# Attention of a decoder step: the scaling of q and k of the later head groups on VectorE, in halves, in place of GpSimd

## Chip, cores and metric

One core of one Trainium2 chip. The metric is the device time of one execution, in microseconds (us); lower is better. The engines are named as in the profile: PE (TensorE matmuls), PEld (its weight loads), DVE (VectorE), ACT (ScalarE), POOL (GpSimd) and SP (SyncE, here only a DMA queue).

## The reference, cut to what matters

The kernel computes one step of a two-layer decoder trunk for 1040 prompt positions (16 meta tokens and 1024 prompt tokens) and 32 sample tokens: a convolution module with its ConvFFN, then multi-head latent attention with its ConvFFN. The change lies in the prompt attention. With 16 heads, queries and keys are projected from small latents, normalised per head, and the queries' last 32 columns are rotated:

```python
q = jnp.einsum('btl,lhd->bthd', rms_norm(xn @ w_dq, q_lat_norm), w_uq)      # 64 + 32 columns a head
q_nope = rms_norm(q[..., :QK_NOPE], qnorm_nope)
q_rope = rope(rms_norm(q[..., QK_NOPE:], qnorm_rope), pos)
k_nope = rms_norm(jnp.einsum('btc,chd->bthd', c, w_uk), knorm_nope)
s = (q_nope . k_nope + q_rope . kr) * SM_SCALE; causal mask; p = softmax(s); o = p @ v
```

The RMS norm of a head is a sum of squares over its 64 (or 32) columns, a reciprocal root `rr`, and a product of the columns with `rr`. That last product, 64 columns by one number for each token and head, is what the change moves. Gains are applied later, at the transposes.

## The kernel before

The trunk runs as stages one after the other: convolution, first ConvFFN, the shared latents, prompt attention (about 1344 to 1760 us in the trace), sample attention, output projection, second ConvFFN.

Prompt attention takes the 16 heads one by one, in four groups of four. For each head `n` the loop at the end of `attention` walks the 14 steps of `values(n, 0)` and `values(n, 1)`: three matmuls give a block of scores (L1349, L1351, L1352), DVE adds the causal mask on the diagonal blocks (L1354), ACT takes the exponential (L1356), two matmuls of one line weigh the values (L1339). Between those steps other generators are advanced a step at a time: `scores(n + 1)`, the row maxima of the next head (PE L1309, DVE L1311, L1314, L1316), `shift(n + 1)` (DVE L1325), `query(n + 1)` (transposes L1279, splits on ACT and DVE, L137 and L138), `keys` (transposes L1257, splits L135 and L136), `inner` (DVE L1294).

The next group of heads is prepared by the generator `side`, advanced 1.3 steps for each step of `values` (`RATE`) from step 8 (`SIDE`) of a group's first head on: `group_k(g + 1)`, then `group_q(g + 1)`. For group 1 `group_q` has already made its ten first steps before the loop. Each of the two projects nine blocks of 128 tokens (the ninth has 64 rows) on PE, copies them and squares them on ACT (L1159, L1161, L1195 to L1198), sums the squares on DVE (L1162, L1202, L1203), takes the root by Newton steps on DVE (`rsqrt`, L255 to L260, giving `rrk` or `rrq`), and then scales, in the three pieces of `PIECES`: blocks 0 to 3, blocks 4 to 7, and block 8.

- In `group_k` the scaling of a piece is one product over 1024 columns on 128 partitions (256 columns on 64 for block 8), L1177, on POOL.
- In `group_q` the inner function `chunk` makes a piece in three steps: the scaling of the 64 plain columns of each head (L1211, by the engine given as `eng`: POOL for the later groups), the scaling of the 32 rotary columns into a scratch tile (L1217, DVE, 512 columns), and the rotation in `rope` (four products L1105 and L1108, L1109, DVE, 256 columns each). The plain and the rotary columns are apart, so L1211 and the DVE operations of the same piece don't wait for each other.

Group 0 goes another way (pieces by pairs of heads, `range(2)` loops), which stays as it is.

`finish(p)` closes a pair of heads: DMAs from POOL's queue (L1380, L1381, L1383, L1385) with a reciprocal on DVE between them (L1382), a product on POOL (L1386) and a DMA (L1387).

The order of instructions on each engine is fixed when the program is built: a planner walks a simulated time line (`schedule_with_timeline_sim`) and takes, on each engine, what is ready in the order of the program text, ahead of its place where the engine would be free. At run time each engine goes through its list in that order. PE's list alone is left as written in a few places outside attention.

Of the kernel before, what the change touches and what calls it, by code (L numbers as in the profile page):

```python
# [12 lines left out]
ALU = mybir.AluOpType  # L13
# [42 lines left out]
INN = 3  # L56
EARLY = 3
PIECES = ((128, 0, 4), (128, 4, 4), (64, 8, 1))
QROW = (96, 0)
SIDE = 8  # L60
FILLQ = 4
# [57 lines left out]
class Prog:  # L119
# [991 lines left out]
    def attention(self, es):  # L1111
        nc, a = self.nc, self.a
# [22 lines left out]
        def sub(t, m, b0, nb, lo, step, w):  # L1135
            v = t[:m, b0:b0 + nb]
            return bass.AP(v.tensor, v.offset + lo, [list(v.ap[0]), [224, 2 * nb], [step, 2], [1, w]])
# [8 lines left out]
        def group_k(g):  # L1146
            kt = st["k"] = st["k"] if g else f32([128, NB, 256], "k", ag)
            uk = part("uk", a["wuk"][:, 256 * g:256 * g + 256], 256)
            ss, rr = f32([128, 36], "ssk", al), f32([128, 36], "rrk", al)
            nc.gpsimd.memset(ss, 1.0)  # L1150
            yield
            for b0 in range(0, NB, 2):
                nb = min(2, NB - b0)
                m = 128 if b0 < 8 else 64
                ps = (ps_p if g else ps_f).tile([128, 512], F32, name="p")[:m, :256 * nb]
                for j in range(nb):
                    c0 = 128 * (b0 + j)
                    self.mm3(ps[:, 256 * j:256 * j + 256], self.cth[:, c0:c0 + m], self.ctl[:, c0:c0 + m], uk[0], uk[1])
                nc.scalar.activation(fl(kt[:m, b0:b0 + nb]), ps, AF.Copy)  # L1159
                sc = f32([128, 1024], "scr", bp)[:m, :256 * nb]  # L1160
                nc.scalar.activation(sc, ps, AF.Square)  # L1161
                nc.vector.tensor_reduce(out=ss[:m, 4 * b0:4 * b0 + 4 * nb], in_=sc.rearrange("p (a b) -> p a b", b=64), op=ALU.add, axis=AX.X)  # L1162
                yield
            self.rsqrt(al, rr, [(ALL, ss, 1.0 / DN)], [128, 36], "ka")
            nc.gpsimd.tensor_copy(self.rnew[:, 4 * g:4 * g + 4], rr[:64, 32:36])
            yield
            for p in () if g else range(2):
                for m, b0, nb in ((64, 8, 1), (128, 0, 8)):
                    v = kt[:m, b0:b0 + nb, 128 * p:128 * p + 128].rearrange("p a (c b) -> p a c b", b=64)
                    s = rr[:m, 4 * b0:4 * b0 + 4 * nb].rearrange("p (a c b) -> p a c b", c=4, b=1)[:, :, 2 * p:2 * p + 2].broadcast_to([m, nb, 2, 64])  # L1170
                    x = (nc.gpsimd if p else nc.vector).tensor_tensor(out=v, in0=v, in1=s, op=ALU.mult)
                    for early in st["half"] if p else ():
                        self.after(x, early)
                yield
            for m, b0, nb in PIECES if g else ():
                v = kt[:m, b0:b0 + nb].rearrange("p a (c b) -> p (a c) b", b=64)
                nc.gpsimd.tensor_tensor(out=v, in0=v, in1=rr[:m, 4 * b0:4 * b0 + 4 * nb].rearrange("p (a b) -> p a b", b=1)  # L1177
                                        .broadcast_to([m, 4 * nb, 64]), op=ALU.mult)
                yield

        def group_q(g):
            q = st["qn"] = f32([128, NB, 2, 224], f"q{g % 2}", au if g % 2 else ag)
# [5 lines left out]
            for b in range(NB):  # L1188
                m = 128 if b < 8 else 64
# [17 lines left out]

            def chunk(v, r, m, b0, nb, c, eng):
                s = lambda i, w: r(i).broadcast_to([m, c * nb // 2, 2, w])
                w = v(0, 160, 64)  # L1210
                x = eng.tensor_tensor(out=w, in0=w, in1=s(0, 64), op=ALU.mult)  # L1211
                for early in st.get("half", ()):
                    self.after(x, early)
                yield
                w = v(64, 64, 32)
                t = f32([128, 1024], "scr", bp)[:m, :32 * c * nb].rearrange("p (a b) -> p a b", b=32)
                nc.vector.tensor_tensor(out=t.rearrange("p (a c) b -> p a c b", c=2), in0=w, in1=s(1, 32), op=ALU.mult)  # L1217
                yield
                st["rope"] = self.rope(f32([128, 1024], "scr", bp), "q", m, slice(b0, b0 + nb), c, w[:, :, :, 0:16], w[:, :, :, 16:32],
                                       t.rearrange("p (a c) b -> p a c b", c=c))  # L1220
                yield

            for r in () if g else range(2):
                for m, b0, nb in ((64, 8, 1), (128, 0, 8)):
                    def v(lo, step, w):
                        x = q[:m, b0:b0 + nb, r]
                        return bass.AP(x.tensor, x.offset + lo, [list(x.ap[0]), [448, nb], [step, 2], [1, w]])
# [3 lines left out]
                yield "half"  # L1231
            for m, b0, nb in PIECES if g else ():
                s = lambda i: rr[:m, i, 4 * b0:4 * b0 + 4 * nb].rearrange("p (a c b) -> p a c b", c=2, b=1)
                yield from chunk(lambda lo, step, w: sub(q, m, b0, nb, lo, step, w), s, m, b0, nb, 4, nc.gpsimd)

        def group_v(g):
            uv = part("uv", a["wuv"][:, 256 * g:256 * g + 256], 256, au)
# [656 lines left out]
```

## Time and profile before

| what | us |
|---|---|
| three runs | 2752.87, 2759.51, 2760.22 |
| median | 2759.51 |
| the profiled execution, whole | 2764.96 |
| its span, first to last instruction | 2763.0 |
| PE busy in it | 2654.5 |
| DVE busy in it | 1879.3 |
| POOL busy in it | 709.8 |

The profile gives, for one execution, every instruction with its start, length and what ended the idle time before it. A line of the kernel is written L1177. Windows give the busy time of each engine in a stretch, and the clock granted to TensorE as a share of 2.4 GHz (0.50 is its lower level, 1.2 GHz). The time line of an engine merges neighbours of one kind ("x3" is three instructions in one row, whose length is from the first's start to the last's end). Instructions of DVE overlap by some 0.07 us, so that the next one may start a little before the end shown for the last.

### The profile page before, as it was taken

How to read it: one execution, taken by the hardware profiler on the slowest of the kernel's cores; microseconds unless marked ns; L12 is line 12 of the kernel's file. 1: busy time of each engine (PE TensorE's matmuls, PEld its weight loads, DVE VectorE, ACT ScalarE, POOL GpSimd, SP SyncE). 2: the span in 40 equal slices, each digit the busy share in tenths (PEclk: the TensorE clock that was granted, in tenths of full speed). 3: DMA queues.
4: the chain of work that ended last, by engine and by line, in shares of the span. 5: the costliest groups of instructions: out<-in, count | busy, mean ns of one | idle time of the engine just before them, and what ended most of it. 6: DMA issues, size and time to landing. Idle time of an engine off the chain costs nothing.

```text
span 2763.0 us, 46569 instructions
## 1 busy us (share of the span) xinstructions
PE 2654.5 (96%) x16966; PEld 2449.1 (89%) x16966; DVE 1879.3 (68%) x3485; ACT 1356.8 (49%) x3701; POOL 709.8 (26%) x1019
## 2 busy tenths in 40 slices
PE   7999998999999999999889999999999999999999
PEld 6888876999999999999767776667999999999999
DVE  8899986578888875145677777676378777775232
ACT  6777775345544553023555555576245454453010
POOL 1567663023332330001111212120023333330000
PEclk9999997999999999999889999999999999999999
DMA  4111101502222236132100001367302222226122
GB/s 142 56 41 55 39 28 43 175 30 92 90 92 91 79 120 229 41 95 92 37 10 19 24 24 32 90 202 261 140 24 90 80 80 81 80 96 244 41 87 76
DMA packets 127770, 238.24 MB, mean 86 GB/s; under 512 B 39779, under 2 KB 81141, under 8 KB 127413
## 3 DMA queue, kind: packets, MB, share of 16 engines
q1 hardware_dynamic: 103828, 200.82, 22.4%
q0 software_dynamic: 9600, 32.36, 3.1%
q10 hardware_dynamic: 14112, 2.09, 0.5%
q8 instruction: 133, 2.18, 0.3%
q14 instruction: 97, 0.79, 0.1%
HBM read 183.90 MB, written 51.31 MB: 85 GB/s over the span
## 4 chain that ended last, share of the span: by engine, by line
PE 84%; DVE 6%; ACT 5%; DMA 2%; issue 2%; SPq 0%; POOL 0%; ACTq 0%; DVEq 0%; POOLq 0%
PE ps L797 29%; PE ps L175 22%; PE pk L654 5%; PE g L419 4%; PE v L1339 4%; PE ps L846 3%; PE p L151 2%; PE ps L197 2%; PE ps L1015 1%; PE p L1349 1%; PE p L1351 1%; PE p L1352 1%; PE po L1653 1%; PE s L1309 1%; PE ps L151 1%
## 5 line engine op out<-in xcount | busy, mean ns | idle before, releaser
L135 ACT ACTIVATE wh<-raw 128x512 fp32r<-128x512 f32 (+2 forms) x256 | 191.1, 749 | 539.7 <-PE ps L175 338.2
L136 DVE TENSOR_TENSOR wl<-raw,wh 128x512 fp32r<-128x512 f32 (+2 forms) x244 | 201.5, 829 | 107.4 <-ACT wh L135 105.1
L944 DVE TENSOR_TENSOR x<-ps,x 128x1074 f32<-128x1074 f32 (+1 forms) x48 | 61.0, 1270 | 291.5 <-PE ps L175 291.3
L767 DVE SCALAR_TENSOR_TENSOR c<-ub,c,c 128x1040 f32<-128x1040 f32 (+1 forms) x176 | 225.3, 1312 | 29.5 <-ACT c L763 28.4
L669 ACT ACTIVATE qq<-pk 128x64 f32<-128x64 f32 x736 | 158.4, 244 | 67.8 <-PE pk L654 67.7
L761 POOL COPY sb<-ub 128x32 f32<-128x32 f32 x88 | 87.6, 997 | 393.3 <-DVE ub L808 353.1
L1339 PE MATMUL v<-pf,vf 128*128 128x512 f32 (+4 forms) x448 | 174.4, 473 | 11.1 <-ACT pf L1356 10.7
L663 POOL TENSOR_TENSOR sq<-sq 128x256 f32<-128x256 f32 (+4 forms) x229 | 140.1, 620 | 102.1 <-ACT sq L658 95.1
L1356 ACT ACTIVATE pf<-p 128x512 f32<-128x512 f32 (+4 forms) x224 | 99.1, 450 | 118.0 <-DVE p L1354 97.4
L175 PE MATMUL ps<-xh,wh 128*128 128x358 f32 (+1 forms) x672 | 148.1, 329 | 9.2 <-ACT xh L135 5.9
L669 ACT ACTIVATION_READ_ACCUMULATOR qq<-pk 128x1 f32 x736 | 154.2, 228 | 0.0
L523 DVE SCALAR_TENSOR_TENSOR a<-u,c,a 128x512 f32<-128x512 f32 x216 | 150.2, 747 | 4.9 <-ACT a L516 4.9
L175 PE MATMUL ps<-xl,wh 128*128 128x358 f32 (+1 forms) x672 | 147.8, 328 | 0.1
L175 PE MATMUL ps<-xh,wl 128*128 128x358 f32 (+1 forms) x672 | 147.3, 327 | 0.0
L175 PE MATMUL ps<-al,wh 128*128 128x358 f32 (+1 forms) x672 | 147.2, 327 | 0.0
L175 PE MATMUL ps<-ah,wl 128*128 128x358 f32 (+1 forms) x672 | 146.5, 326 | 0.0
L175 PE MATMUL ps<-ah,wh 128*128 128x358 f32 (+1 forms) x672 | 146.2, 326 | 0.0
L654 PE MATMUL pk<-ukh,ch 128*128 128x512 f32 x256 | 115.3, 451 | 26.1 <-ACT ch L135 13.6
L763 ACT ACTIVATE c<-ub,c 128x1074 f32<-128x1074 f32 (+1 forms) x88 | 101.5, 1187 | 60.0 <-DVE ub L808 46.3
L175 PEld LDWEIGHTS ps<-xh,wh 128*128 128x128 f32 x672 | 117.2, 191 | 12.8 <-ACT xh L135 6.8
L658 ACT ACTIVATE sq<-pk 128x512 f32<-128x512 f32 x164 | 99.8, 613 | 50.3 <-PE pk L654 47.5
L135 ACT ACTIVATE wh<-s 128x512 fp32r<-128x512 f32 x120 | 75.6, 630 | 93.5 <-PE ps L797 86.7
(599 smaller groups left out, 9111.5 us busy)
## 6 DMA issues: line engine op xcount, KB each, us to landing
raw<-wup SPq DMA_DIRECT2D x88, 512.0 KB, 3.6
pg<-ctn SPq DMA_DIRECT2D x128, 192.0 KB, 3.8
raw<-wdn SPq DMA_DIRECT2D x32, 448.0 KB, 3.4
raw<-pw SPq DMA_DIRECT2D x24, 512.0 KB, 3.9
d_a<-c POOLq DMA_DIRECT2D x22, 537.0 KB, 3.5
raw<-d_a SPq DMA_DIRECT2D x22, 537.0 KB, 5.1
d_a<-c POOLq DMA_DIRECT2D x22, 531.0 KB, 3.2
raw<-d_a SPq DMA_DIRECT2D x22, 531.0 KB, 5.3
```

The costliest lines, as they stand in the source:

```text
L135: return (nc.scalar.activation(h, src, AF.Copy), (eng or nc.vector).tensor_tensor(out=l, in0=src, in1=h.bitcast(F32), op=ALU.subtract))
L136: (eng or nc.vector).tensor_tensor(out=l, in0=src, in1=h.bitcast(F32), op=ALU.subtract))
L175: nc.tensor.matmul(p[:, c, :ch], s[:, k * 128:(k + 1) * 128], m[k][:, off + c * ch:off + (c + 1) * ch], start=k == 0 and i == 0, stop=k == ...
L419: y = nc.tensor.matmul(p[:, 0], x[:, k * 128:(k + 1) * 128], m[k][:, t * ch:t * ch + ch], start=k == 0 and i == 0, stop=k == KD - 1 and i ...
L523: nc.vector.scalar_tensor_tensor(out=p[:, :ND] if j == n - 1 else acc, in0=x[:, j:j + ND], scalar=w[:, j:j + 1], in1=to if j == 1 else acc ...
L654: x = nc.tensor.matmul(ps, s[:, j, :], m[:, 512 * c:512 * c + 512], start=i == 0, stop=i == 2)
L663: nc.gpsimd.tensor_tensor(out=to, in0=v[:, :, :n], in1=v[:, :, n:2 * n], op=ALU.add)
L669: nc.scalar.activation(q, ps[:, 64 * h:64 * h + 64], AF.Square, accum_out=ss[:, p, 8 * c + h:8 * c + h + 1])
L763: x = nc.scalar.activation(c, ub, AF.Copy, scale=wd[:, t, 2:3])
L767: nc.vector.scalar_tensor_tensor(out=c[:, 2:pe], in0=ub[:, tap:tap + pe - 2], scalar=wd[:, t, tap:tap + 1], in1=c[:, 2:pe], op0=ALU.mult, ...
L797: nc.tensor.matmul(ps, w[:, s], m[:, lo:hi], start=first and k == 0 and i == 0, stop=k == KD // 2 - 1 and i == 2, skip_group_check=True)
L1339: nc.tensor.matmul(o[:, at_:], vf[:m, b, c], p[:m, :512 - at_], start=b == 0, stop=last)
```

## The change

The three pieces of the key scaling become five (blocks 0 and 1, 2 and 3, 4 and 5, 6 and 7, 8), on DVE, each a step of the generator. The scaling of the plain query columns goes to DVE too; its pieces of four blocks are cut into two instructions of 512 columns, with the generator's step between the two, and the step that stood after the scaling falls away for these pieces, so that the second half and L1217 stand in one step. Group 0, and the last block of the later groups, keep one instruction and their steps. The keys of a group now take two steps more in `side`, the queries as many as before.

```diff
+HALVES = ((128, 0, 2), (128, 2, 2), (128, 4, 2), (128, 6, 2), (64, 8, 1))
...
-            for m, b0, nb in PIECES if g else ():
+            for m, b0, nb in HALVES if g else ():
                 v = kt[:m, b0:b0 + nb].rearrange("p a (c b) -> p (a c) b", b=64)
-                nc.gpsimd.tensor_tensor(out=v, in0=v, in1=rr[:m, 4 * b0:4 * b0 + 4 * nb].rearrange("p (a b) -> p a b", b=1)
+                nc.vector.tensor_tensor(out=v, in0=v, in1=rr[:m, 4 * b0:4 * b0 + 4 * nb].rearrange("p (a b) -> p a b", b=1)
                                         .broadcast_to([m, 4 * nb, 64]), op=ALU.mult)
                 yield
...
             def chunk(v, r, m, b0, nb, c, eng):
                 s = lambda i, w: r(i).broadcast_to([m, c * nb // 2, 2, w])
-                w = v(0, 160, 64)
-                x = eng.tensor_tensor(out=w, in0=w, in1=s(0, 64), op=ALU.mult)
+                w, z = v(0, 160, 64), s(0, 64)
+                n = c * nb // 2
+                for lo, hi in ((0, n // 2), (n // 2, n)) if c == 4 and nb > 1 else ((0, n),):
+                    if lo:
+                        yield
+                    x = eng.tensor_tensor(out=w[:, lo:hi], in0=w[:, lo:hi], in1=z[:, lo:hi], op=ALU.mult)
                 for early in st.get("half", ()):
                     self.after(x, early)
-                yield
+                if c == 2 or nb == 1:
+                    yield
...
             for m, b0, nb in PIECES if g else ():
                 s = lambda i: rr[:m, i, 4 * b0:4 * b0 + 4 * nb].rearrange("p (a c b) -> p a c b", c=2, b=1)
-                yield from chunk(lambda lo, step, w: sub(q, m, b0, nb, lo, step, w), s, m, b0, nb, 4, nc.gpsimd)
+                yield from chunk(lambda lo, step, w: sub(q, m, b0, nb, lo, step, w), s, m, b0, nb, 4, nc.vector)
```

For the later groups `st["half"]` is empty, so no added edge hangs on these instructions.

## Rows read from the trace of the kernel before

**Rows 1.** Page, busy time of each engine, share, instructions

```profile
PE 2654.5 (96%) x16966; PEld 2449.1 (89%) x16966; DVE 1879.3 (68%) x3485; ACT 1356.8 (49%) x3701; POOL 709.8 (26%) x1019
```

**Rows 2.** Page, the chain that ended last, by engine

```profile
PE 84%; DVE 6%; ACT 5%; DMA 2%; issue 2%; SPq 0%; POOL 0%; ACTq 0%; DVEq 0%; POOLq 0%
```

**Rows 3.** Windows: length, busy PE, PEld, DVE, ACT, POOL, clock, DMA share, GB/s

```profile
1440.00:1465.00 25.00, 23.04 (x111) 16.04 (x110) 21.39 (x80) 13.18 (x31) 5.15 (x6) 1.00 0.02 6
...
1540.00:1570.00 30.00, 29.59 (x152) 23.60 (x151) 21.09 (x90) 19.24 (x54) 5.27 (x7) 1.00 0.00 1
1570.00:1600.00 30.00, 25.31 (x116) 17.70 (x115) 27.82 (x87) 14.03 (x32) 11.56 (x12) 0.94 0.12 37
...
1680.00:1700.00 20.00, 16.41 (x59) 10.76 (x59) 17.71 (x49) 5.52 (x14) 10.14 (x11) 0.83 0.10 28
```

**Rows 4.** Time line of POOL: start, length, instruction [idle before, releaser]

```profile
1421.65 4.33 POOL L1211 TENSOR_TENSOR q<-q,rrq 128x1024 f32<-128x1024 f32 x3 [12.16 <-DVE rrq L260]
...
1458.98 4.33 POOL L1177 TENSOR_TENSOR k<-k,rrk 128x1024 f32<-128x1024 f32 x3
...
1575.42 5.24 POOL L1211 TENSOR_TENSOR q<-q,rrq 128x1024 f32<-128x1024 f32 x3 [0.36 <-DVE mx L1316]
1580.61 0.58 POOL L1383 DMA_DIRECT2D d_l<-lq  x1
...
1587.51 2.37 POOL L1386 TENSOR_TENSOR o<-o,lb 128x1024 f32<-128x1024 f32 x1 [3.85 <-DMA lb<-d_l]
...
1682.59 4.33 POOL L1211 TENSOR_TENSOR q<-q,rrq 128x1024 f32<-128x1024 f32 x3
```

**Rows 5.** Time line of DVE after the queries' root of group 2

```profile
1575.43 0.67 DVE L1217 TENSOR_TENSOR scr<-q,rrq 128x512 f32<-128x512 f32 x1
...
1577.02 1.13 DVE L1105 TENSOR_TENSOR scr<-scr,tabqcos 128x256 f32<-128x256 f32 x1
1578.08 2.87 DVE L1105 TENSOR_TENSOR scr<-scr,tabqsin 128x256 f32<-128x256 f32 x2
1580.87 0.41 DVE L1105 TENSOR_TENSOR scr<-scr,tabqcos 128x256 f32<-128x256 f32 x1
1581.20 0.17 DVE L1354 TENSOR_TENSOR p<-p,trit 128x16 f32<-128x16 f32 x1
...
1585.07 0.75 DVE L1105 TENSOR_TENSOR scr<-scr,tabqsin 128x256 f32<-128x256 f32 x2
...
1588.50 1.66 DVE L1109 TENSOR_TENSOR q<-scr 128x256 f32<-128x256 f32 x1
```

**Rows 6.** Time line of DVE after the queries' root of group 3

```profile
1682.74 4.74 DVE L1217 TENSOR_TENSOR scr<-q,rrq 128x512 f32<-128x512 f32 x1
```

**Rows 7.** Time line of PE: the long idle times of groups 2 and 3

```profile
1581.65 0.40 PE L1339 MATMUL v<-pf,vf 128*128 128x16 f32 x2 [2.90 <-ACT pf L1356]
...
1687.68 0.50 PE L1349 MATMUL p<-qh,kth 104*128 104x512 f32 x1 [2.41 <-DVE s L1294]
```

**Rows 8.** Windows of 1 us after each of those idle times, columns as above

```profile
1583.00:1584.00 1.00, 1.00 (x4) 0.47 (x2) 1.00 (x3) 0.95 (x3) 0.66 (x2) 0.50 0.21 29
...
1691.00:1692.00 1.00, 1.00 (x3) 0.81 (x4) 1.00 (x3) 0.98 (x3) 0.00 (x0) 0.50 0.04 8
```

**Rows 9.** Time line of DVE: the whole-piece scaling in group 0

```profile
1388.40 1.21 DVE L1211 TENSOR_TENSOR q<-q,rrq 128x1024 f32<-128x1024 f32 x1
```

**Rows 10.** Windows of 5 us around the preparation of group 1, columns as above

```profile
1430.00:1435.00 5.00, 5.00 (x26) 3.48 (x24) 2.17 (x7) 2.84 (x7) 0.00 (x0) 1.00 0.00 0
...
1445.00:1450.00 5.00, 4.10 (x19) 2.89 (x19) 5.00 (x19) 3.11 (x8) 0.68 (x2) 1.00 0.01 3
1450.00:1455.00 5.00, 4.26 (x25) 3.24 (x24) 5.00 (x20) 1.08 (x4) 0.00 (x0) 1.00 0.07 24
```

**Rows 11.** Time line of DVE: idle times after the keys' roots (groups 1, 2)

```profile
1465.94 0.17 DVE L1354 TENSOR_TENSOR p<-p,trit 16x16 f32<-16x16 f32 x1 [1.80 <-PE p L1352]
...
1556.01 0.48 DVE L1202 TENSOR_REDUCE ssq<-scr 128x2 f32<-128x128 f32 x2 [1.67 <-ACT scr L1198]
```

## Prediction

> **What bounds the kernel now.** I read the page's busy shares first, then its chain, then windows over prompt attention, then the time lines of POOL, DVE and PE where a window shows PE short of work. PE is busy for 96% of the span [rows 1] and holds 84% of the chain [rows 2], so a change on DVE and POOL is worth only what PE's idle times, or its clock, have to do with those engines. The windows show where that is [rows 3]. While the keys of group 2 are made, PE is busy for 29.59 of 30 us. In the next 30 us, where group 2's queries are scaled and rotated, PE has 25.31 and the mean clock falls to 0.94; in the 20 us where group 3's are, it has 16.41 at a clock of 0.83. Idle time there is 4.7 and 3.6 us, and the lowered clock is worth 30 x 0.06 = 1.8 and 20 x 0.17 = 3.4 us: 13.5 us in all, the most that could be won in these two places. In both, DVE is nearly full (27.82 of 30, 17.71 of 20).
>
> Why DVE is full there is seen in its time line beside POOL's. In group 3 one L1217 of 512 columns takes 4.74 us [rows 6]; its twin in group 2 takes 0.67 [rows 5]. The long one lies over POOL's three L1211, 4.33 us from 1682.59 on [rows 4]. In group 2 the same POOL work starts at 1575.42, just ahead of a chain of L1105: one of 1.13 us and a pair of 2.87, where a clean single takes 0.41 and a clean pair 0.75 [rows 5]. So DVE's products whose two inputs both lie in SBUF stand still while POOL's products run: 4.74 - 0.67 = 4.07 us in group 3, (1.13 - 0.41) + (2.87 - 0.75) = 2.84 us in group 2. Behind them in DVE's list stands a causal mask (L1354 at 1581.20) or an `inner` (L1294), for which PE waits by way of the exponential or directly: its 2.90 and 2.41 us of idle time [rows 7]. After each, the clock stands at 0.50, the lower of its two levels, for some microseconds [rows 8]. The keys' scalings (L1177) and group 1's queries, as long on POOL [rows 4], run where PE has no such gap.
>
> **The change part by part.**
>
> *Removed from POOL:* L1177 and L1211 of three groups, about six times 4.33 us [rows 4]. POOL is busy for 26% [rows 1] and none of that is on the chain [rows 2], so its own time is worth nothing. What counts is the standstill of DVE: 2.84 + 4.07 = 6.9 us.
>
> *Added to DVE:* a whole piece takes 1.21 us there [rows 9]; a half of 512 columns is priced by L1217, 0.67 us, and the 256 columns of the last block by L1105, 0.41 us [rows 5]. Keys: 4 x 0.67 + 0.41 = 3.1 us a group; queries the same. That is 6.2 us a group and 18.5 us in all, 2.7 times the standstill removed. The added work is worse for DVE's total; it has to be won by place.
>
> The two instructions of a pair cost 1.34 against 1.21 us, 0.13 us more. The Trainium skill, VectorE: DVE Perf Modes, section The TRN2 errata, says that VectorE pays a fixed latency for each instruction, so that small tiles pay more often: that speaks against halves, and 12 pairs at 0.13 make the 1.6 us already in the 18.5.
>
> *Group 2's queries.* Ahead of the late mask now stand the first piece's two halves, 1.34 us, in place of 2.84 us of standstill: the mask is 1.5 us earlier, and of PE's 2.90 us about 1.4 stay. The second piece and the small one, 1.34 + 0.41 = 1.75 us, come later in a stretch where DVE is still behind; between nothing and 1.75 I take 0.5, since PE is busy again there.
>
> *Group 3's queries.* 4.07 - 1.34 = 2.7 us earlier, more than the 2.41 us of PE's wait, so I count 2.4; what is late next is the mask after it, and again 0.5 of 1.75 for the rest.
>
> How long this standstill is decides the sum. The row has it as long as all three POOL products. The Trainium skill, SBUF — State Buffer, section SBUF: two separate sides, says that a VectorE instruction with two SBUF inputs and a GpSimd instruction that reads SBUF lock each other out, whoever starts first holding the ports for its whole instruction. By that L1217 should have waited for one product, not three; at a third of 4.33 us group 3 would gain nearly nothing, and my sum would be 2 us less. The row decides.
>
> *The clock.* If the idle times shrink, the fall after them may not come: between 0 and 1.8 us in group 2, 0 and 3.4 in group 3. In group 2 a gap of half the length stays, so 0; in group 3 I take half, 1.7.
>
> *Keys of groups 2 and 3.* 3.1 us each, at a time when PE is full and DVE has 21.09 of 30 us [rows 3], with idle times such as 1.67 us just behind [rows 11]. Cover: those gaps, some 9 us in the window. Without it, masks and row maxima queue behind the scalings, and the price is the whole 3.1. In halves no mask waits for more than 0.67 us at once. I take 0.3 each, bounds 0 and 3.1.
>
> *Group 1, keys and queries.* Here DVE is tightest: from 1445 to 1455 it has no idle time and PE already loses 0.90 + 0.74 us [rows 10]. The query scalings are ready early (POOL begins at 1421.65 [rows 4]) and DVE has 2.83 us free of 5 at 1430 [rows 10], so the planner can set them there. The keys' come at 1459 [rows 4], with a gap of 1.80 us soon after [rows 11]. Together 21.39 + 6.2 = 27.6 us stand against a window of 25 [rows 3]. Bounds 0 and 6.2; I take 1.0, nearer to the free ends.
>
> *POOL's queue.* L1383 of `finish` stands behind the L1211 of group 2 until 1580.61; with these gone it goes some 3 us sooner, and L1386 (2.37 us), a product like the others, comes forward. It stops DVE now as well (an L1109 of 1.66 us where 0.41 is usual, at 1588.50 [rows 5]); moved onto other products with two SBUF inputs it can cost up to 2.37 instead of 1.25, or nothing: -1.25 to +1.1 us, taken as 0.
>
> *Steps.* Two more steps of `side` at 1.3 a step move the queries of a group back by 1.5 steps of some 14 a head; they are needed some ten steps later, so that costs nothing unless they become the last thing `query` waits for.
>
> *Sum:* -1.5 + 0.5 - 2.4 + 0.5 - 1.7 + 0.6 + 1.0 = -3.0 us. The profiled execution is 2763.0 us of span and 1.96 outside, 2764.96, which is 5.45 above the median of the three runs, 2759.51. It would come to 2762; against the median the forecast is 2756.5.
>
> **The rivals.**
>
> *The clock stays up.* Both idle times go far enough that no fall follows: -1.5 - 2.4 - 1.8 - 3.4 and no cost of the keys, -9.1 us, 2750.4. For it: the falls come right behind these two idle times and nowhere in the 1540 to 1570 window [rows 3, 8]. Against: the 1.4 us that stay in group 2, and that the scalings themselves now stand on the path.
>
> *DVE takes over (slower).* In each head that prepares a group, the added products stand ahead of masks in a list that runs in order; PE waits for masks through ACT. It decides when the gaps of DVE are not where the planner puts the halves, which shows first in group 1, where 27.6 us stand against 25. If all of it were exposed: 18.5 - 6.9 = +11.6 us, 2771; if two thirds, +8 and 2767. For it: DVE is already full beside PE's small losses at 1445 to 1455 [rows 10]. Against: the 9 us free in 1540 to 1570.
>
> *The loss only changes its name.* The masks now wait for scalings on DVE instead of a standstill, and L1386 lands worse: -1.5 - 2.4 + 3.5 + 1.6 + 1.1 = about +2 us, 2762. For it: DVE's total rises.
>
> *The planner's order turns elsewhere.* A change of engine alters its simulated time line, and lists further on may be set otherwise: no row prices this; I give it -10 to +10, nearest to the 5 us that single stalls are worth here.
>
> **How the numbers follow.** A measurement of this kernel tells about 0.3% from no change, 8.3 us: faster means below 2751.2, slower above 2767.8. The forecast has 0.52 (its own range 2751 to 2763), the clock 0.16, DVE taking over 0.16, the renamed loss 0.10, the planner 0.06. Faster: 0.12 of the clock's, 0.04 of the forecast's, 0.03 of the planner's, 0.19. Slower: 0.11 of DVE's, 0.03 of the planner's, 0.01 of the renamed loss, 0.15. The rest is 0.66. The range leaves out the outer parts of the two far cases: 2747 to 2768.
>
> **What would show it.** Right: no L1217 or L1105 of over 1 us beside L1211; the idle times before L1339 and L1349 in groups 2 and 3 under 1.5 us; clock above 0.9 in group 3's window; DVE's busy time up by about 18.5 - 6.9 = 11.6 us; POOL's down by 26. Wrong: masks that wait for DVE in heads 0 and 1, where group 1 is made, PE idle times of over 1 us there or beside the keys, or query transposes that come later than the rotation allowed before. A change of over 10 us in either direction would mean that the planner moved work that I have not looked at.

## The result, and the profile of the changed kernel

| | before | changed |
|---|---|---|
| median of 22 runs each, us | 2758.23 | 2761.61 |
| lowest to highest, us | 2751.60 to 2764.65 | 2755.34 to 2771.07 |
| profiled execution, us | 2764.96 | 2771.07 |
| its span, us | 2763.0 | 2769.2 |

The ratio is 1.0018, with an interval of 1.0010 to 1.0026: by it the changed kernel is 2.8 to 7.2 us slower (the medians differ by 3.4). That is less than the 0.3% I had named as the measurement's limit, but the sign is plain by this interval, and it is not the sign of the forecast, -3.0 us. How far such an interval holds from one set of runs to the next is seen below, at the kernel that was run two times. The profiled execution of the changed kernel is the slowest of its 22.

Lines behind the change stand six further on (L1360 for L1354, L1331 for L1325), those just ahead of it one (L1106 for L1105) and L1211 is L1216. The page of the changed kernel, busy times and the chain, against [rows 1, 2]:

```profile
PE 2655.6 (96%) x16966; PEld 2449.3 (88%) x16966; DVE 1889.6 (68%) x3515; ACT 1357.2 (49%) x3701; POOL 683.7 (25%) x1001
...
PE 81%; DVE 7%; ACT 5%; DMA 3%; issue 2%; POOL 0%; SPq 0%; ACTq 0%; DVEq 0%; POOLq 0%
```

DVE is busy for 10.3 us more (11.6 expected), POOL for 26.1 less (26 expected). So the work moved as priced, and the standstill went with it. The time line of DVE in the changed kernel, after the root of group 2's queries, against [rows 5]:

```profile
1584.40 1.29 DVE L1216 TENSOR_TENSOR q<-q,rrq 128x512 f32<-128x512 f32 x2
1585.61 0.69 DVE L1223 TENSOR_TENSOR scr<-q,rrq 128x512 f32<-128x512 f32 x1
1586.21 1.62 DVE L1216 TENSOR_TENSOR q<-q,rrq 128x512 f32<-128x512 f32 x3
...
1588.78 0.41 DVE L1106 TENSOR_TENSOR scr<-scr,tabqcos 128x256 f32<-128x256 f32 x1
...
1590.91 2.58 DVE L1109 TENSOR_TENSOR q<-scr 128x256 f32<-128x256 f32 x1
...
1600.32 1.20 DVE L1331 TENSOR_TENSOR qh<-p,pick 8x1024 fp32r<-8x1024 f32 x1
...
1604.85 0.22 DVE L1109 TENSOR_TENSOR q<-scr 64x64 f32<-64x64 f32 x1
1604.99 0.21 DVE L1110 TENSOR_TENSOR q<-scr 64x64 f32<-64x64 f32 x1
```

The L1106 has its clean 0.41 us where before it took 1.13. All five scalings of the plain query columns (L1216, two and three) stand in one stretch of 3.4 us with one L1223 between them, though the generator's steps lie between them in the program: the planner drew them together, so the halves spread nothing here. One standstill remains: an L1109 of 2.58 us, under `finish`'s product on POOL, 1.66 before [rows 5]. New is the end of the list. The last rotation product of the group starts at 1604.99, 4.7 us *behind* the `shift` (L1331, 1600.32) of the head that runs then; before, it started 3.1 us ahead of that `shift`:

```profile
1592.02 0.21 DVE L1109 TENSOR_TENSOR q<-scr 64x64 f32<-64x64 f32 x1
...
1595.16 1.20 DVE L1325 TENSOR_TENSOR qh<-p,pick 8x1024 fp32r<-8x1024 f32 x1
```

`shift` marks each head once, so the time from one `shift` to the next is the time of a head. I count heads from 0 and call "head 6" the time from the seventh `shift` to the eighth. Heads 2, 3, 8, 12 and 13 repeat within 0.1 us in most kernels, which makes these times a finer measure than the whole. Head 4 takes 27.5 or 27.9 us in most, and head 14, from 25.4 to 30.0 us, is left out. In us:

| head | 0 | 1 | 4 | 5 | 6 | 7 | 9 | 10 | 11 | 0 to 13 |
|---|---|---|---|---|---|---|---|---|---|---|
| before | 25.2 | 23.8 | 27.5 | 30.0 | 27.5 | 22.7 | 30.0 | 28.7 | 22.7 | 355.2 |
| changed | 26.7 | 24.8 | 27.9 | 30.9 | 25.6 | 25.4 | 30.2 | 25.2 | 25.4 | 359.1 |

The standstills lay in heads 6 and 10. These won 1.9 and 3.6 us. Heads 7 and 11, right behind, lost 2.7 and 2.7, heads 5 and 9 lost 0.9 and 0.2, and heads 0 and 1, where group 1 is made, 1.5 and 1.0. The profiled executions differ by 6.2 us. Of this 3.9 lie here. Another 3.4 lie ahead of the first `shift`: the shared latents start 5.5 us later in the changed kernel's execution, though up to attention every engine has the same instructions in the same order, so that this part is no effect of the change. From the end of head 13 to 1960 us of the kernel before, from where on the lists are the same again, the changed kernel takes 3.2 us more, and behind that 4.2 less.

What makes heads 7 and 11 longer is the clock. First windows of the kernel before, from head 6's standstill and then from head 7 (columns as in [rows 3]):

```profile
1578.00:1583.00 5.00, 2.10 (x10) 1.53 (x9) 5.00 (x12) 1.59 (x4) 3.58 (x4) 0.97 0.01 2
1583.00:1588.00 5.00, 5.00 (x13) 3.02 (x12) 3.67 (x13) 1.82 (x4) 1.16 (x3) 0.69 0.43 107
...
1595.00:1600.00 5.00, 3.98 (x24) 2.89 (x21) 4.94 (x15) 3.92 (x9) 0.08 (x1) 1.00 0.01 3
1600.00:1605.00 5.00, 4.70 (x27) 3.68 (x28) 3.50 (x17) 1.72 (x7) 0.42 (x1) 1.00 0.00 1
```

And the changed kernel, two windows of head 6, then two of head 7, and two of head 11:

```profile
1585.00:1590.00 5.00, 5.00 (x20) 3.44 (x19) 5.00 (x13) 3.07 (x6) 1.06 (x2) 1.00 0.37 108
1590.00:1595.00 5.00, 4.25 (x16) 2.36 (x14) 5.00 (x11) 1.10 (x3) 3.24 (x2) 1.00 0.06 25
...
1600.00:1605.00 5.00, 3.66 (x16) 2.83 (x15) 4.81 (x13) 2.19 (x5) 0.50 (x1) 0.78 0.00 0
1605.00:1610.00 5.00, 4.45 (x13) 2.59 (x11) 2.86 (x12) 2.44 (x6) 0.00 (x0) 0.54 0.02 4
...
1709.00:1714.00 5.00, 3.76 (x15) 2.68 (x15) 4.81 (x17) 2.93 (x7) 0.51 (x1) 0.80 0.00 1
1714.00:1719.00 5.00, 4.99 (x15) 3.04 (x15) 2.33 (x10) 1.34 (x5) 0.00 (x0) 0.52 0.00 0
```

The hole of 2.90 us is gone and the clock of head 6 stays at 1.00. In head 7, PE now has 3.66 of 5 us and the clock falls to 0.78 and then 0.54; 5 x 0.22 + 5 x 0.46 = 3.4 us of full clock are lost there, and before none. PE's time line of the changed kernel shows what it lacks ahead of that fall, and the twin in head 11:

```profile
1595.18 0.66 PE L1263 MATMUL s<-c,k 128*128 128x128 f32 x4 [0.93 <-DVE m L1320]
...
1601.58 0.50 PE L1355 MATMUL p<-qh,kth 128*128 128x512 f32 x1 [1.34 <-DVE qh L1331]
...
1710.02 0.51 PE L1355 MATMUL p<-qh,kth 128*128 128x512 f32 x1 [1.34 <-DVE qh L1331]
```

Both are waits for DVE, for a row maximum and for the `shift` itself. In DVE's list both stand behind rotation products of this group, whose end now reaches into the next head. That these waits bring the fall is argued and not shown: in the kernel with group 1 as before, below, PE waits the same 1.34 us for the `shift` in head 11, the rotation ends 4.7 us behind that `shift` as well, and the clock of the head stays at 1.00.

### The profile page after: what moved, and what is told of

It is laid out like the page before. It is cut to its first block, busy times and chain, and to the rows that moved or that the text cites. A ratio compares the mean times of both kernels' runs of the same rounds, so it can differ in the third digit from the quotient of the medians.

```text
span 2769.2 us, 46583 instructions
## 1 busy us (share of the span) xinstructions
PE 2655.6 (96%) x16966; PEld 2449.3 (88%) x16966; DVE 1889.6 (68%) x3515; ACT 1357.2 (49%) x3701; POOL 683.7 (25%) x1001
## 4 chain that ended last, share of the span: by engine, by line
PE 81%; DVE 7%; ACT 5%; DMA 3%; issue 2%; POOL 0%; SPq 0%; ACTq 0%; DVEq 0%; POOLq 0%
PE ps L798 27%; PE ps L176 22%; PE pk L655 5%; PE g L420 4%; PE v L1345 4%; PE ps L847 3%; PE p L152 2%; PE ps L198 2%; PE ps L1016 1%; PE p L1355 1%; PE p L1358 1%; PE p L1357 1%; PE s L1315 1%; PE po L1659 1%; PE ps L152 1%
## 5 line engine op out<-in xcount | busy, mean ns | idle before, releaser
L768 DVE SCALAR_TENSOR_TENSOR c<-ub,c,c 128x1040 f32<-128x1040 f32 (+1 forms) x176 | 225.6, 1314 | 30.9 <-ACT c L764 30.1
```

What stands on the lines that cost most here:

```text
L768: nc.vector.scalar_tensor_tensor(out=c[:, 2:pe], in0=ub[:, tap:tap + pe - 2], scalar=wd[:, t, tap:tap + 1], in1=c[:, 2:pe], op0=ALU.mult, ...
```

## The experiments

Three theories stood at the start. A: the loss moved from POOL's standstill to DVE's own added work at the end of a group. B: the two steps added to `side` by cutting the keys' scaling in five push the queries' root back, by 2.9 us, into the next head's work. C: group 1 pays.

The table has the time of heads, the start of the queries' root (last line of `rsqrt`) counted from the `shift` that opens head 5 (9), and the ratio to the kernel before with its interval. All from one profile each but the ratio. "Halves" and "whole" say how VectorE's scalings are cut.

| kernel | 1 | 5 | 6 | 7 | 9 | 10 | 11 | 0 to 13 | root g2, g3 | ratio |
|---|---|---|---|---|---|---|---|---|---|---|
| before | 23.8 | 30.0 | 27.5 | 22.7 | 30.0 | 28.7 | 22.7 | 355.2 | 37.4, 36.5 | |
| changed | 24.8 | 30.9 | 25.6 | 25.4 | 30.2 | 25.2 | 25.4 | 359.1 | 40.3, 39.6 | 1.0018 (1.0010 to 1.0026) |
| keys only | 24.6 | 30.8 | 26.6 | 27.1 | 30.2 | 26.8 | 24.7 | 361.9 | 40.2, 39.6 | 1.0035 (1.0022 to 1.0048) |
| queries only | 23.8 | 30.0 | 26.3 | 22.7 | 30.1 | 26.0 | 27.4 | 357.5 | 37.5, 36.6 | 1.0005 (0.9996 to 1.0015) |
| group 1 as before | 23.8 | 30.8 | 25.2 | 26.5 | 30.2 | 25.1 | 23.1 | 355.6 | 40.2, 39.6 | 1.0003 (0.9994 to 1.0012) |
| whole, steps of before | 24.7 | 30.0 | 26.4 | 22.7 | 31.1 | 24.3 | 23.2 | 353.8 | 37.4, 37.6 | 0.9991 (0.9980 to 1.0002) |
| two empty steps | 23.8 | 30.8 | 26.6 | 24.6 | 30.2 | 26.8 | 24.7 | 358.5 | 40.2, 39.6 | 1.0035 (1.0023 to 1.0047) |
| halves, three steps | 24.8 | 30.0 | 28.0 | 22.7 | 30.9 | 24.4 | 23.2 | 355.6 | 38.9, 37.4 | 1.0039 (1.0026 to 1.0052) |
| the same again | 24.8 | 30.0 | 26.3 | 22.7 | 30.9 | 24.4 | 23.2 | 353.7 | 37.5, 37.4 | 1.0007 (0.9994 to 1.0020) |
| RATE 1.39 | 24.6 | 30.2 | 26.2 | 22.7 | 31.0 | 24.4 | 23.2 | 355.8 | 37.6, 37.5 | 0.9998 (0.9988 to 1.0008) |
| whole, one key step | 24.7 | 34.2 | 25.0 | 22.7 | 33.4 | 25.0 | 22.7 | 359.2 | 30.9, 29.5 | 1.0010 (0.9999 to 1.0021) |
| whole, groups 2 and 3 | 23.8 | 30.0 | 26.2 | 22.7 | 30.7 | 24.3 | 23.2 | 352.1 | 37.4, 37.2 | 0.9982 (0.9971 to 0.9992) |
| RATE 1.39, group 1 as before | 23.8 | 30.2 | 26.2 | 22.7 | 31.0 | 24.4 | 24.8 | 356.0 | 37.7, 37.5 | 0.9993 (0.9981 to 1.0005) |
| no plain scaling | 24.0 | 30.0 | 23.9 | 22.7 | 30.0 | 23.3 | 22.7 | 348.2 | 37.4, 36.5 | 0.9957 (0.9944 to 0.9970) |

**Keys only** (the changed kernel with the queries back on POOL):

```diff
-                for lo, hi in ((0, n // 2), (n // 2, n)) if c == 4 and nb > 1 else ((0, n),):
+                for lo, hi in ((0, n // 2), (n // 2, n)) if eng is not nc.gpsimd and c == 4 and nb > 1 else ((0, n),):
...
-                if c == 2 or nb == 1:
+                if eng is nc.gpsimd or c == 2 or nb == 1:
...
-                ... s, m, b0, nb, 4, nc.vector)
+                ... s, m, b0, nb, 4, nc.gpsimd)
```

> Only the keys' scaling of the later groups goes to VectorE in five instructions; the queries' stays on GpSimd as before. Theory A (the loss moved: the changed kernel wins some 1.9 and 3.6 us where GpSimd no longer stops VectorE's rotation, in heads 6 and 10, and gives back 2.7 us in each of the heads 7 and 11, because the queries' products now end later on VectorE than the transposes that need them): the keys alone cost little, within 1.5 us of before, the long L1217 and L1105 beside GpSimd's L1211 are still there, and heads 7 and 11 take as long as before (22.7 us from shift to shift). Theory B (the two more steps that the keys take push the queries back): heads 7 and 11 lose some 2.7 us each here too, 4 to 6 us over before. Theory C (group 1 is the dearer part): 1 us or more is lost in head 1 by its keys.

It is slower than the whole change. The root comes 2.8 us later in group 2, and the standstill of [rows 5] is back, in DVE's time line:

```profile
1582.39 1.26 DVE L1106 TENSOR_TENSOR scr<-scr,tabqcos 128x256 f32<-128x256 f32 x1
1583.57 2.87 DVE L1106 TENSOR_TENSOR scr<-scr,tabqsin 128x256 f32<-128x256 f32 x2
```

So the half of the change that I had priced at 0.6 us for two groups carries the loss, and it is found in heads 7 and 11 again. That fits B, and speaks against A, by which the queries' scalings should be the dear ones.

**Queries only** (the changed kernel with the keys as before: `PIECES`, on POOL, three steps):

```diff
-            for m, b0, nb in HALVES if g else ():
+            for m, b0, nb in PIECES if g else ():
...
-                nc.vector.tensor_tensor(out=v, in0=v, in1=rr[:m, 4 * b0 ...
+                nc.gpsimd.tensor_tensor(out=v, in0=v, in1=rr[:m, 4 * b0 ...
```

> Only the queries' plain columns of the later groups go to VectorE in halves; the keys' scaling stays on GpSimd in three pieces with three steps. Theory A: all of the changed kernel's pattern is here, heads 6 and 10 shorter by 1.9 and 3.6 us than before, heads 7 and 11 longer by 2.7 each, group 1's query products in head 0 costing some 1.5 us; 2 to 5 us over before in all. Theory B: with the steps as before the queries come in time, heads 7 and 11 are as before, and the kernel is 2 to 4 us faster than before.

The root is back in place, and group 2 gains: head 6 1.2 us less, head 7 unchanged. Group 3 doesn't: head 10 wins 2.8 us and head 11 loses 4.7, though its root is where it was before. In time it is level with the kernel before, where B wanted 2 to 4 us less and A 2 to 5 more. In PE's time line there:

```profile
1706.88 0.50 PE L1355 MATMUL p<-qh,kth 128*128 128x512 f32 x1 [2.32 <-DVE qh L1331]
```

This head is A's case, and B doesn't explain it. The fall of the clock right behind that idle time, to 0.70 and 0.50 in windows of 5 us, comes with most of its price.

**Group 1 as before** (in the changed kernel, `g > 1` decides between the new form and the old; `chunk` as in keys only):

```diff
-            for m, b0, nb in HALVES if g else ():
+            for m, b0, nb in (HALVES if g > 1 else PIECES) if g else ():
...
-                nc.vector.tensor_tensor(out=v, ...
+                (nc.vector if g > 1 else nc.gpsimd).tensor_tensor(out=v, ...
...
-                ... s, m, b0, nb, 4, nc.vector)
+                ... s, m, b0, nb, 4, nc.vector if g > 1 else nc.gpsimd)
```

> The changed kernel with group 1's keys and queries left on GpSimd in whole pieces; groups 2 and 3 as changed. Theory C (group 1 pays: its query products stand ahead of masks in head 0 while TensorE's clock is still at its lower level, and its keys fill VectorE in head 1): 2.5 us are won back against the change, so about 2 us over before, and the clock from 1420 to 1430 us is as before. Theory A alone: the same 2.5 us, with heads 6, 7, 10 and 11 as in the changed kernel. If group 1 costs nothing: as the changed kernel, 5 us over before.

Head 1 is at 23.8 us again, so C has a size: 1.0 us there. It stands or goes with the keys' scaling of group 1 in all 13 profiles with the whole work (24.6 to 24.8 with it on VectorE, 23.8 without). Head 0 can't be charged: it takes 26.2 to 26.9 us in every kernel but the one before (25.2), those included that leave group 1 alone. Head 11 is an exception to B: its root is as late as in the changed kernel, and it is 0.4 us over before.

**Whole pieces, steps of before** (the kernel before, only the two engine names changed):

```diff
-                nc.gpsimd.tensor_tensor(out=v, in0=v, in1=rr[:m, 4 * b0 ...
+                nc.vector.tensor_tensor(out=v, in0=v, in1=rr[:m, 4 * b0 ...
...
-                ... s, m, b0, nb, 4, nc.gpsimd)
+                ... s, m, b0, nb, 4, nc.vector)
```

> Both scalings on VectorE, but in whole pieces of four blocks with the steps of before: three steps for the keys, one product of 1024 columns (1.21 us) for a pair of halves (1.34 us). Theory A: as the changed kernel, 3 to 6 us over before; longer products ahead of masks cost about what the saved 1.6 us give. Theory B: with the steps as before heads 7 and 11 lose nothing and the kernel is 1 to 3 us below before.

The same work on the same engine as in the change, without its steps: head 6 wins 1.1 us, head 10 4.4, heads 7 and 11 lose 0 and 0.6, head 9 1.1. In time it is level with the kernel before or a little better. A is refuted as the main cause: the added DVE work as such doesn't make the kernel slower.

**Two empty steps** (the kernel before, with two steps added that do nothing):

```diff
                                         .broadcast_to([m, 4 * nb, 64]), op=ALU.mult)
                 yield
+                if b0 < 8:
+                    yield
```

> The kernel before, GpSimd and all, with nothing added but two empty steps in each later group's keys, so that the projections of the queries start 1.5 steps of the values later. Theory B: the root of the queries is 2.9 us later after the shift of head 5 and heads 7 and 11 lose some 2 to 4 us each against before: 4 to 9 us over before without any work moved. Theory A: within 1.5 us of before.

Nothing is moved to VectorE, and the kernel is as slow as with the keys' half of the change: 6.3 to 13 us by its interval, which is of one set of six runs. Heads 5, 9 and 11 have the change's times or nearly (30.8, 30.2, 24.7), head 7 is 2.0 us up. Windows behind the `shift` of head 7 and of head 11 in this kernel:

```profile
1593.00:1598.00 5.00, 3.60 (x18) 2.64 (x19) 4.69 (x11) 3.78 (x10) 0.27 (x1) 1.00 0.01 3
1598.00:1603.00 5.00, 5.00 (x21) 3.55 (x20) 2.92 (x12) 1.30 (x5) 0.23 (x1) 0.66 0.00 1
...
1707.00:1712.00 5.00, 4.94 (x19) 3.56 (x20) 2.79 (x14) 1.55 (x5) 0.47 (x1) 0.66 0.01 1
```

The clock falls to 0.66 in each. So two steps without any work bring the fall to these heads, and this is B by itself. It also corrects a reading: heads 6 and 10 are 0.9 and 2.0 us *shorter* here, with the products still on POOL, so a part of what the changed kernel won there was only put off into the next head. Over the whole of these two heads the clock is 1.00 here and was 0.94 and 0.88 before, with the standstill in both kernels. From the start of head 5 to the end of head 11 the two steps cost 2.0 us; of the 3.3 over attention, 1.0 lies in head 0, which can't be charged.

The wait at the end of head 6 can be followed. In the time lines of POOL, DVE and PE:

```profile
1585.51 2.34 POOL L1388 TENSOR_TENSOR o<-o,lb 128x1024 f32<-128x1024 f32 x1 [3.53 <-DMA lb<-d_l]
```

```profile
1585.92 2.21 DVE L1108 TENSOR_TENSOR q<-scr 128x256 f32<-128x256 f32 x1
...
1588.26 0.51 DVE L1316 TENSOR_REDUCE m<-s 128x1 f32<-128x352 f32 x1
...
1590.99 0.21 DVE L1109 TENSOR_TENSOR q<-scr 64x64 f32<-64x64 f32 x1
...
1592.64 1.20 DVE L1327 TENSOR_TENSOR qh<-p,pick 8x1024 fp32r<-8x1024 f32 x1
```

```profile
1588.82 0.65 PE L1259 MATMUL s<-c,k 128*128 128x128 f32 x4 [1.96 <-DVE m L1316]
```

The delayed rotation product L1108 (clean 0.41 us) is held under `finish`'s product on POOL, the row maximum comes behind it, and PE stands for 1.96 us. The rotation itself ends 1.6 us *ahead* of the `shift` here: the late root brings the loss without the rotation reaching into the next head.

**Halves, in three steps** (the changed kernel, the halves of one piece in one step), run two times:

```diff
-                yield
+                if b0 not in (0, 4):
+                    yield
```

> The changed kernel with the keys' five products in three steps instead of five: a step stands behind each pair of halves and behind the small piece, as before the change. Theory B (the two added steps push the queries' root back by 1.5 steps of the values, 2.9 us, and their products past the transposes of the next group): the queries' root comes some 37.5 us after the shift of head 5 (40.3 in the changed kernel), the rotation ends at about 53 us instead of 61, heads 7 and 11 lose under 1 us, and the kernel is 1 to 3 us below before, like the kernel with whole pieces. Theory A (the added products on VectorE fill the end of the group whatever the steps): heads 7 and 11 together still lose 4 us or more, and it stays 4 to 6 us over before.

> The run of three key steps once more, the same kernel: it was timed 10.7 us over the kernel before, of which its profile has only 0.4 inside attention. If the rest lies in a stage order that this kernel always has, 2767 us again, ratio 1.004, and 159 to 160 us from the last shift to the end of the first part of sample attention where before has 155. If it was the spread from execution to execution, within 3 us of before, ratio 1.000 to 1.001.

Heads 7 and 11 are back at 22.7 and 23.2 in both, which B wants. The first time the kernel was timed 10.7 us over the one before, the second time 2 us (-1.7 to +5.5). The two intervals don't meet, so an interval of one set of runs is narrower than the spread between sets; the times of "keys only" and of the two empty steps, of five and six runs that were not repeated, are to be read with that, and the argument goes by the heads. The profiles, 14.7 us apart as a whole, show one source of the spread, 1.9 us of it. One program, and in head 6 the windows of the first profile, then those of the second:

```profile
1574.00:1578.00 4.00, 3.28 (x11) 1.98 (x10) 2.23 (x11) 1.77 (x5) 1.08 (x2) 0.68 0.01 1
...
1586.00:1590.00 4.00, 4.00 (x9) 2.12 (x9) 4.00 (x14) 1.67 (x3) 1.05 (x2) 0.62 0.47 131
```

```profile
1569.00:1573.00 4.00, 3.27 (x18) 2.15 (x17) 3.32 (x19) 2.54 (x7) 1.08 (x2) 1.00 0.01 1
...
1581.00:1585.00 4.00, 4.00 (x15) 2.37 (x14) 4.00 (x15) 0.60 (x1) 0.48 (x1) 1.00 0.48 124
```

PE is as busy in the one as in the other (3.28 and 3.27, then 4.00 and 4.00 of 4 us), and the clock falls in one alone: 28.0 against 26.3 us for the head, which is most of the 1.9. A single head time of a single profile is therefore good to some 1.7 us where a fall is near, not to 0.1. What carries B is the count. In the four kernels with the late root (39.6 to 40.3 us), seven of the eight heads 7 and 11 are 1.9 us or more over before; in the eight other profiles with the whole work, whose root is at its old place within 1.5 us or earlier, it is two of sixteen (head 11 of "queries only" and of the RATE kernel with group 1 as before).

**RATE 1.39** (the changed kernel; `side` goes faster, so that five steps take no longer than three did), and **with group 1 as before** on top:

```diff
-RATE = 1.3
+RATE = 1.39
```

> The changed kernel with the generator advanced 1.39 steps for each step of the values in place of 1.3, so that its 32 steps take the time that 30 took. Theory B: the root of the queries is back at about 37.5 us after the shift of head 5, and the 5 us of the change are won back: between 3 us below and 1 over before. Theory A: still 4 to 6 us over before.

> The changed kernel with group 1 back on GpSimd and RATE 1.39 in place of 1.3, so that the keys' five steps take no longer than three did. Theory B and C: heads 0 and 1 as before, heads 7 and 11 at 22.7 and 23.3 us as in the run with RATE 1.39 alone, about 353.5 us from first to last shift, 1.7 us under the kernel before: ratio 0.9994. Theory A: heads 7 and 11 stay near 25.4 us, ratio 1.001.

The root is back at 37.6 and the loss in heads 7 and 11 with it (22.7, 23.2), in the first; in time it is the kernel before again, since heads 4 and 8 pay 1.5 and 0.5 us for the faster `side`. In the second, head 11 had a fall of the clock once more, and the gain that I expected over the first is within the interval. As a number it is a miss, 356.0 us for 353.5.

**Whole pieces, keys in one step** (the kernel with whole pieces and the steps of before, with two steps fewer):

```diff
-                yield
+                if b0 == 8:
+                    yield
```

> Whole pieces on VectorE for both, and the three products of the keys in one step instead of three, two steps fewer than before. Theory B carried on: the queries' root comes another 2.9 us sooner, 34.5 us after the shift of head 5, and the end of the group gets slack: 2 to 6 us below before. If the steps of before are already early enough: as with whole pieces, 1 to 3 us below before; if the three products of the keys in one place stand ahead of masks, up to 2 us worse than that.

Earlier isn't better either, and the expectation missed: the root comes at 30.9 and 29.5 us for the 34.5 expected, the time is +2.8 us (-0.3 to +5.8) for -2 to -6, heads 6 and 11 are as short as in any kernel with the whole work, but heads 5 and 9 pay 4.2 and 3.4 us for the work that now falls into them.

**No plain scaling.** The kernel before without the product L1211 of groups 1 to 3; what it computes for these heads lacks that factor.

```diff
-                x = eng.tensor_tensor(out=w, in0=w, in1=s(0, 64), op=ALU.mult)
+                if c == 2:
+                    x = eng.tensor_tensor(out=w, in0=w, in1=s(0, 64), op=ALU.mult)
```

> The kernel before without the scaling of the plain query columns of groups 1 to 3 (left out altogether, on GpSimd as on VectorE), its steps kept: what the change could win at most at the queries if VectorE's halves cost nothing. All theories: the standstills go, heads 6 and 10 fall by 2 and 4 to 5 us; B says that heads 7 and 11 stay at 22.7, so 348 to 350 us from first to last shift against 355.2, ratio 0.9975 to 0.998. If heads 7 and 11 rise here as well, the loss there isn't from VectorE's work or the steps but from what follows when the standstill goes.

This is the ceiling: heads 6 and 10 fall by 3.6 and 5.5 us and heads 7 and 11 don't move, 7.0 us over attention and 8 to 15 in time, more than the 5.5 to 7 expected. Taking the standstill away has no loss of its own behind it.

**Whole pieces, groups 2 and 3 alone** (steps of before, group 1 on POOL):

```diff
-                nc.gpsimd.tensor_tensor(out=v, in0=v, in1=rr[:m, 4 * b0 ...
+                (nc.vector if g > 1 else nc.gpsimd).tensor_tensor(out=v, in0=v, in1=rr[:m, 4 * b0 ...
...
-                ... s, m, b0, nb, 4, nc.gpsimd)
+                ... s, m, b0, nb, 4, nc.vector if g > 1 else nc.gpsimd)
```

> The kernel before, with the scalings of keys and queries of groups 2 and 3 alone as whole pieces on VectorE, one step each as before; group 1 stays on GpSimd. Theory B and C together (the lock at the queries costs, the added steps and group 1's move give the gain back): heads 0 and 1 as before (25.2 and 23.8 us from shift to shift), heads 6 and 10 as in the run of whole pieces for all groups (26.4 and 24.3 us against 27.5 and 28.7), 352.3 us from first to last shift against 355.2, so 2.5 to 3 us under the kernel before: ratio 0.999. Theory A (the added VectorE work costs at the group's end whatever the steps): 355 us or more, ratio 1.000 to 1.002.

Expected were 352.3 us over attention, found 352.1; the median of 12 runs is 2751.55 us, the ratio 0.9982 (0.9971 to 0.9992). By its interval, of one set of runs, it is faster than the kernel before, by 5 us, and its ratio lies below the changed kernel's. The end of its rotation and the next `shift` in DVE's time line, and windows of its head 7:

```profile
1590.49 1.75 DVE L1105 TENSOR_TENSOR scr<-scr,tabqcos 64x64 f32<-64x64 f32 x1
...
1593.35 0.20 DVE L1109 TENSOR_TENSOR q<-scr 64x64 f32<-64x64 f32 x1
...
1596.98 1.20 DVE L1325 TENSOR_TENSOR qh<-p,pick 8x1024 fp32r<-8x1024 f32 x1
```

```profile
1597.00:1602.00 5.00, 3.81 (x23) 2.83 (x21) 4.94 (x15) 3.99 (x10) 0.25 (x1) 1.00 0.02 3
1602.00:1607.00 5.00, 4.87 (x27) 3.81 (x28) 3.43 (x18) 1.65 (x7) 0.25 (x1) 1.00 0.00 1
```

The rotation ends 3.6 us ahead of the `shift`, much as before, and the clock holds. In group 3 it ends 1.6 us ahead, no more than with the two empty steps, and the clock of head 11 holds as well.

## Why the prediction was wrong

**The step that failed** is "Steps". It had the size right: 1.5 steps, and the root came 2.9 us later in group 2 (40.3 against 37.4). It priced them at nothing, since the queries "are needed some ten steps later". That looked at when the queries are needed, and not at where their products stand in DVE's list. The runs give the price. From the start of head 5 to the end of head 11 the kernel before takes 189.3 us and the changed kernel 190.4. The same halves with the keys in three steps, and so with the root in its place, take 186.9 and 185.3, and with five steps and a faster `side` 186.0. So the two steps cost 3.4 to 5.1 us in these heads, where the rest of the change won 2.4 and 4.0. In the kernel before, without any work moved, they cost 2.0.

How the late root costs that is shown in part only. In the changed kernel the rotation ends 4.7 us behind the `shift` of head 7, where before it ended 3.1 ahead, with DVE at 27.82 of 30 us [rows 3]. But a used-up slack is not what the late kernels share: with keys only and with two empty steps the rotation ends 1.6 us ahead of the `shift`, as it does ahead of that of head 11 in five profiles whose clock holds there. What the four share, in both groups, is the product that `finish` holds up: one of 256 columns on 128 partitions, for 2.2 to 2.6 us. With the whole work and the root in its old place it is one of 64 columns on 64 partitions, for 1.1 to 2.0 us (in group 2 of the kernel before one of 256, for 1.66), and with the keys in one step none. No run moves the one without the other, and head 11 of "group 1 as before" has both and no fall. What the falls in heads 7 and 11 hang on stays open.

**The removed standstill** came out in size, but not as reckoned. With the steps as before, VectorE's scalings make head 6 shorter by 1.1 to 1.3 us (but for the profile with the fall of the clock) and head 10 by 2.8 to 4.4; the sum had 1.0 for group 2 and 2.4 - 0.5 + 1.7 = 3.6 for group 3. Of that, PE's idle time in the two heads was to fall by 2.9 us and fell by 1.9 (8.4 before, 6.5 in the second profile with halves in three steps), and the clock was counted with 1.7 and gave more: 0.94 and 0.88 over the two heads before, worth 1.7 and 3.4 us, and 1.00 in both after. The two empty steps raise it to 1.00 there with the standstill in place, so that the clock's part can't be put down to the standstill, and that the total fits is partly luck. Whether one instruction waits for one POOL product or for several stays with [rows 6]: where the standstill is back, in "keys only", three L1106 share 2.97 us of it, which either reading allows. Not every product stands still: in [rows 5] the L1217 that starts together with POOL's three has its clean 0.67 us, and POOL's three take 5.24 us there for 4.33 elsewhere [rows 4]. The Trainium skill, SBUF — State Buffer, section SBUF: two separate sides, has the one who comes first hold the ports for its whole instruction; the collision with `finish`, under POOL's queue below, agrees, since DVE's product there ends 0.27 us behind POOL's.

**The clock** was right in its place and wrong in its account. The falls in heads 6 and 10 did go, but I counted 1.7 us as won without asking where PE would be short next. They came back one head later, at 0.54 and 0.52. All the signs named for "right" came (the products clean, PE's idle times before those two lines under 1.5 us, DVE up by 10.3 and POOL down by 26.1 us), because they look at heads 6 and 10 alone.

**Keys of groups 2 and 3**: 0.3 each was taken, and the scaling itself costs head 5 nothing: 30.0 us with whole pieces on VectorE, 30.8 with two empty steps and no scaling. The 0.9 in head 5 are the steps again. In head 9 the scalings cost 0.7 to 1.1 us in the kernels without added steps or with the faster `side`, and with the late root 0.2, as much as the two empty steps without them.

**Group 1**: 1.0 us taken, 1.0 measured in head 1. That the queries' part is free couldn't be settled, since head 0 varies. In the changed kernel's time line of DVE they stand ahead of the maxima in one block, a stretch in which the clock was low already:

```profile
1425.71 2.21 DVE L1216 TENSOR_TENSOR q<-q,rrq 128x512 f32<-128x512 f32 x4
```

**POOL's queue**: taken as 0 between -1.25 and +1.1. It went to the dear end. POOL's product of `finish` in the changed kernel,

```profile
1590.58 2.64 POOL L1392 TENSOR_TENSOR o<-o,lb 128x1024 f32<-128x1024 f32 x1 [3.60 <-DMA lb<-d_l]
```

covers the L1109 of 2.58 us: 2.17 over its clean 0.41, for 1.25 before, so +0.9. The one ends at 1593.22, the other at 1593.49.

**Halves or whole** made no difference that shows: 353.7 and 353.8 us over attention with the steps of before (355.6 in the halves' other profile, with the fall in head 6). The 1.6 us for more instructions were too small to matter.

**The rivals.** "The loss only changes its name" came nearest, with +2 us and the collision with `finish`; its mechanism, masks behind the scalings, is not what the runs show, as whole pieces without the steps have no such loss. "DVE takes over" is refuted as a matter of total work: the same work gains when its place is kept. "The clock stays up" held in heads 6 and 10 and failed one head on. "The planner's order turns elsewhere" is not excluded: PE's and DVE's lists differ from those of before on into sample attention, to some 1947 us, and the changed kernel's 3.2 us behind head 13 lie there; but the two profiles of one program (halves in three steps) differ by 4.0 in that stretch. The sum without the failed step was -3.0; kernels with that work and the old steps measured -1.5 (whole), +0.4 and -1.5 (halves) over attention, and -3.2 without group 1.

**Still open** is why the times of whole runs differ by more than attention does. The two empty steps cost 9.7 us in time (6.3 to 13) and 3.3 over attention; the kernel without plain scaling won 12 and 7.0. One profile each can't tell, since the first matmul of the shared latents alone starts between 1299.4 and 1306.2 us in the 14 profiles, with an order of instructions up to there that is the same in all. Head 11 of "queries only" is open too.

## What to carry to other kernels

Adding a `yield` to a generator that fills the gaps of another loop is a change of place for everything that follows in it, and so has a price of its own. Before calling it free, read in the trace where the delayed chain will stand: how far its last instruction is ahead of the next work on the same engine, whether that engine is full in between, and which of its instructions will then meet one of another engine that holds it up. A gain in one stretch is booked only when the next stretch has been asked what it will be short of; and moving work to another engine and moving it in time are best tried apart.

## What the hardware showed that I had not expected

The same program, with PE as busy in the windows concerned, kept its clock at 1.00 in one execution and fell to 0.68 and 0.62 in another; 1.7 us in one head. And one product of POOL (L1386 in the fastest kernel with the whole work, 2.35 us from 1589.81 on) held a product of DVE of only 64 x 64 elements, the L1105 of 1.75 us shown there, where its twins take some 0.2: what such a collision costs goes by what is left of POOL's instruction, however small DVE's is.
